# Changing the issue order of weight products, weight splits and one root in a decoder trunk on one core

## The chip, the cores and the metric

The kernel runs on one core of one Trainium2 chip. The metric is the device time of one execution in microseconds (us). Five engines matter here: PE (TensorE, matrix products), DVE (VectorE), ACT (ScalarE), POOL (GpSimd) and SP (SyncE), which issues most transfers. Each engine takes its instructions in the order in which the program was laid out for it.

## What is computed

A trunk of four decoder layers serves 256 prompt tokens and 8 x 4 sample tokens with the same weights, 288 token columns in all. Each layer is a feed-forward part, a token mixer and a second feed-forward part, each behind an RMS norm:

```python
for i in range(DEPTH):                       # 4 layers, mixer kind i % 3
    x = x + 0.5 * _swiglu(_rmsnorm(x, ...), ffn_w_in[i, 0], ffn_w_out[i, 0])
    h = _rmsnorm(x, norm_mix[i])
    # 0: sliding-window attention  1: gated delta net  2: gated linear recurrence (HGRN2)
    x = x + y
    x = x + 0.5 * _swiglu(_rmsnorm(x, ...), ffn_w_in[i, 1], ffn_w_out[i, 1])
```

The linear recurrence (layer 2) has 8 heads of width 128. Per head it computes decayed scores inside chunks of 32 tokens, carries a 128 x 128 state from chunk to chunk, and then normalises the head's output: `o * rsqrt(mean(o*o) + eps)`. All numbers are fp32; inputs and outputs are the trunk's rows, caches and states.

## The kernel before

**Weight products.** Activations lie transposed in SBUF, 128 features on the partitions and 288 tokens in the columns. Every weight matrix streams from HBM once, in chunks of 512 rows by 256 columns (four `raw` buffers). To keep fp32 accuracy with fp32r products, each 128-column piece of a chunk is split into a high part (`hi`, ACT, line 71) and the rest (`lo`, DVE, line 72); at most three pieces are split at a time. The activations are split in the same way. A job then covers up to four 128 x 128 blocks, and each block takes three products into the same PSUM tile: hi x high part of the activations (line 97), hi x low part (line 98), lo x high part (line 99). I call these the weight products: a job of four blocks has twelve, two blocks have six. `Stream.run` (line 85) emits the jobs; `Stream.split_to` (line 58) emits the splits two jobs ahead.

**Who decides the order.** The kernel is written against a scheduler that lays out each engine's queue when the program is built: it simulates the engines, and whenever an engine is free it takes the ready instruction of the best priority. Priority is the order of writing, and `tc.high_priority(n)` moves what is written under it n places ahead. `PRIO` is 5000 (line 107). So a weight product can be followed on PE by any other work that is ready and comes earlier in priority. On the chip the order is fixed: an instruction that waits holds up everything behind it on its engine.

**The mixers.** Their own work (scores, transposes, states) mixes with the weight products on PE. In attention (`swa`, line 398) it is written in the evacuations of the q jobs, so it precedes later products. In the recurrence (`hgrn`, line 1281) the 64 jobs of the input projections are written first, with the groups q0, f0, v0, f1, q1, v1, z0, z1 of four heads each; then `head_scores`, `head_states` and `gate` of the heads under `tc.high_priority(PRIO)`, then 8 output jobs after each half of the heads. The splits in this part have the priority of their place, because `st.first`, the places that line 70 moves them ahead, is 0. In the first part of the delta net it is `2 * PRIO`.

**Head norm.** In `head_states` ACT squares the head's output out of a PSUM tile with tag `c1` (line 1483), DVE makes mean plus eps (`gv`, line 1485), `root` (line 274) raises it to -0.5 on POOL (`gf`, one instruction, line 276), and ACT scales the output with it (line 1488), which also frees the PSUM tile. A second way to the same root exists, `rsqrt` (line 264): a bit trick and three Newton steps, two plus nine instructions on DVE, each of which reads what the one before it wrote. The feed-forward norms use it.

**The end of the recurrence.** `gate` (line 1503) multiplies each head's output with its gate z and splits the product for the output projection, whose 16 jobs are the last of this mixer.

```python
with self.tc.high_priority(self.first):                       # splits, line 70
    self.nc.scalar.activation(out=h, in_=src, func=AF.Copy)
...
for i, (xh, xl) in enumerate(xs):                             # products, line 96
    mm(ps, hi[:, i, :m], xh(), start=start and i == 0, stop=False)
    mm(ps, hi[:, i, :m], xl(), start=False, stop=False)
    self.mms.append(mm(ps, lo[:, i, :m], xh(), ...).ins)
```

Of the kernel before, what the change touches and what calls it, by code (L numbers as in the profile page):

```python
# [24 lines left out]
class Stream:  # L25
# [3 lines left out]
    def __init__(self, tc, raw, split, psum):  # L29
        self.tc, self.nc, self.raw, self.split_pool, self.psum = tc, tc.nc, raw, split, psum  # L30
        self.chunks, self.jobs = [], []
        self.loaded, self.tiles, self.left = 0, {}, {}
        self.nsplit, self.parts = 0, {}
        self.njob = 0
        self.accs = {}
        self.pooled = set()
        self.held, self.mms, self.tags = [], [], {}
        self.loads = {}
        self.first = 0

    def chunk(self, loads):
        self.chunks.append(loads)
# [42 lines left out]
    def run(self, count, hold=False):  # L85
        self.mms = []
        for j in range(self.njob, self.njob + count):
            self.split_to(j + 1 + AHEAD)
            chunk, view, nk, xs, acc, start, stop, evac, m = self.jobs[j]
            hi, lo = self.parts.pop(j)  # L90
            if start:
                self.accs[acc] = self.psum.tile([128, 512], F32, tag=self.tags.pop(acc, "acc"), name="acc")
            ps = self.accs[acc][:m, :T]
            mm = self.nc.tensor.matmul
            last = len(xs) - 1
            for i, (xh, xl) in enumerate(xs):
                mm(ps, hi[:, i, :m], xh(), start=start and i == 0, stop=False)  # L97
                mm(ps, hi[:, i, :m], xl(), start=False, stop=False)  # L98
                self.mms.append(mm(ps, lo[:, i, :m], xh(), start=False, stop=stop and i == last).ins)  # L99
            self.njob += 1  # L100
            if stop and hold:
                self.held.append((evac, self.accs.pop(acc)))
            elif stop:
                evac(self.accs.pop(acc))


PRIO = 5000
# [4 lines left out]
def trunk(ctx: ExitStack, tc: tile.TileContext, I, consts, O):  # L112
# [16 lines left out]
    st = Stream(tc, raw, split, Acc)  # L129
# [134 lines left out]
    def rsqrt(r, v, t):  # L264

        ri = r.bitcast(I32)
        V.tensor_single_scalar(ri, v.bitcast(I32), 1, ALU.logical_shift_right)
        V.tensor_scalar(ri, ri, -1.0, 1597463007.0, ALU.mult, ALU.add)
        for _ in range(3):
            V.scalar_tensor_tensor(out=t, in0=r, scalar=-0.5, in1=r, op0=ALU.mult, op1=ALU.mult)  # L270
            V.tensor_tensor(out=t, in0=t, in1=v, op=ALU.mult)
            V.scalar_tensor_tensor(out=r, in0=t, scalar=1.5, in1=r, op0=ALU.add, op1=ALU.mult)

    def root(r, v):

        G.tensor_tensor(out=r, in0=v, in1=roots[:v.shape[0]].to_broadcast(list(v.shape)), op=ALU.pow)  # L276
# [48 lines left out]
    def norm_run(key, halved):  # L325

        st.run(NJ, True)
        mms = st.mms
        with tc.high_priority(N1):
            if key[0] == "f" or key[1] in WIDE:  # L330
                with tc.issue_after(mms[NF]):
                    norm(key, halved)
            else:
                with tc.issue_after(mms[N0[0]]):
                    stats(key)
                newton(key)
                with tc.issue_after(mms[N0[1]]):
                    bcast(key, halved)
        st.flush()
# [941 lines left out]
    def hgrn(i, j):  # L1281
# [3 lines left out]
        q, k, f, z = (Slabs(F32) for _ in range(4))  # L1285
# [157 lines left out]
        def head_states(h):  # L1443

            H = L.pop(("h", h))
            sta, qb, bd, qm = H["sta"], H["qb"], H["bd"], H["qm"]
            vt = L["vt", h // 4][:, h % 4]
            s0 = slice(32 * (h % 4), 32 * (h % 4) + 32)
            vm = mx(1024, "vm", 1).rearrange("p (c n v) -> p c n v", c=2, n=4)
            SS = mx(1024, "SS", 2).rearrange("p (n v) -> p n v", n=8)  # L1450
            for c in range(2):
                for a in range(4):
                    S.activation(out=vm[:, c, a], in_=vt[:, c], func=AF.Copy, scale=L["blk"][:, a:a + 1])
            v4m = mx(1024, "v4m", 1, dt=F32R).rearrange("p (b v) -> p b v", b=8)
            for e in range(8):
                S.activation(out=v4m[:, e], in_=L["v4"][:, h], func=AF.Copy, scale=cc["m8"][:, e:e + 1])
            for c in range(2):
                ps = misc(("c1", "s")[c])
                PE.matmul(ps, H["kdt"][:, c * 128:c * 128 + 128], vm[:, c].rearrange("p n v -> p (n v)"))
                for a in range(4):  # L1460
                    n = 4 * c + a
                    if n == 0:
                        V.tensor_copy(out=SS[:, 0], in_=ps[:, 0:128])
                    else:
                        V.scalar_tensor_tensor(out=SS[:, n], in0=SS[:, n - 1], scalar=H["end"][:, n:n + 1],
                                               in1=ps[:, a * 128:a * 128 + 128], op0=ALU.mult, op1=ALU.add)
            nc.sync.dma_start(out=O[6][j, 0, h], in_=SS[:, 7])
            po = misc("c1")
            for c in range(2):
                PE.matmul(po[:, c * 128:c * 128 + 128], bd[:, c * 128:c * 128 + 128], vt[:, c], start=c == 0, stop=False)  # L1470
                for a in range(4):
                    n = 4 * c + a
                    if n:
                        PE.matmul(po[32 * a:32 * a + 32, c * 128:c * 128 + 128], qb[:, 32 * n:32 * n + 32], SS[:, n - 1],  # L1474
                                  start=False, stop=False)
            for e in range(8):
                a = e % 4
                PE.matmul(po[32 * a:32 * a + 32, 256:384], qm[:, 32 * e:32 * e + 32], sta[:, e], start=False, stop=False)
            PE.matmul(po[:, 256:384], bd[s0, 256:384], L["vs"][s0, h // 4], start=False, stop=True)
            ssq, v, r = sm(3, "gs"), sm(3, "gv"), sm(3, "gf")  # L1480
            o = mx(384, "o", 1)
            for c in range(3):
                S.activation(out=o[:, c * 128:c * 128 + 128], in_=po[:, c * 128:c * 128 + 128], func=AF.Square,
                             accum_out=ssq[:, c:c + 1])
            V.tensor_scalar(v, ssq, 1.0 / 128, EPS, ALU.mult, ALU.add)
            root(r, v)
            for c in range(3):
                S.activation(out=o[:, c * 128:c * 128 + 128], in_=po[:, c * 128:c * 128 + 128], func=AF.Identity,
                             scale=r[:, c:c + 1])
            for e in range(0, 8, 4):  # L1490
                ps = misc(("c1", "s")[e // 4])
                PE.matmul(ps, H["k4"], v4m[:, e:e + 4].rearrange("p b v -> p (b v)"))
                for a in range(4):
                    V.scalar_tensor_tensor(out=sta[:, e + a], in0=sta[:, e + a], scalar=H["ends"][:, (e + a) // 2, a % 2:a % 2 + 1],
                                           in1=ps[:, a * 128:a * 128 + 128], op0=ALU.mult, op1=ALU.add)
            nc.sync.dma_start(out=O[11][j, :, h].rearrange("b k v -> k b v"), in_=sta)
            ps = misc("s")
            for c in range(2):
                PE.transpose(ps[:, c * 128:c * 128 + 128], o[:, c * 128:c * 128 + 128], ident)
            PE.matmul(ps[:, 256:T], o[:, 256:384], L["lm"][:, 5])  # L1500
            S.activation(out=q[h], in_=ps[:, :T], func=AF.Identity, scale=hnorm)
# [19 lines left out]
        def run():  # L1521
            setup()
            norm_run(key, False)
            st.run(64 - NJ)
            for a in (0, 4):
                with tc.high_priority(PRIO):
                    if a == 0:
                        head_scores(0)
                    for h in range(a, a + 4):
                        if h < 7:  # L1530
                            head_scores(h + 1)
                        head_states(h)
                        gate(h)
                st.run(8)
        return run
    rows_y, turned = ((0, 128, 0), (128, 128, 0), (160, 128, 96)), {}

# [108 lines left out]
    ps = misc()  # L1646
# [11 lines left out]
    for k in range(9):  # L1658
        add_square(seq[0], k, G)
    for k, run in zip(seq, runs):  # L1660
        if k[0] == "f":
            run()
        else:
            with tc.tile_pool(name="mix", bufs=1, reuse_waits="tile") as M[0]:
                run()
# [92 lines left out]
```

## Time and profile before

| what | value |
|---|---|
| median of 3 runs | 2639.22 us (2635.47 to 2645.3) |
| the profiled execution's own time | 2632.71 us |
| its span, first to last instruction | 2630.9 us |
| mean granted TensorE clock | 0.989 of 2.4 GHz |
| attention of layer 0, delta net, recurrence, attention of layer 3 | about 228 to 345, 715 to 1150, 1620 to 1850, 2285 to 2400 us |

Engine rows of the profile's page give the busy time, its share of the span and the instructions. Matmuls overlap in the pipeline, so the time from the start of one product to the start of the next says more than the duration of one. Idle time of an engine is listed with what ended it. Clock shares are of 2.4 GHz; 0.5 is the lower level, 1.2 GHz.

### The profile page before, as it was taken

To read this page: it belongs to the slowest core of one execution; us is meant where nothing else is said; L and a number is where in the kernel's file an instruction comes from. 1 tells how busy PE (TensorE), PEld (TensorE's weight loads), DVE (VectorE), ACT (ScalarE), POOL (GpSimd) and SP (SyncE) were. 2 spreads that over 40 slices of the span, in tenths; PEclk is the share of its full clock that TensorE was granted. 3 is DMA by queue.
4 is the path that set the end of the run, shared out by engine and by line. 5 is a ranking of instruction groups with operands and counts; after the bars stand their busy time and mean duration, and the time that the engine had idled before them with its cause. 6 is when DMAs were issued, how large, how long until landed. Compare 5 with 4: busy or idle time off the path is not lost.

```text
span 2630.9 us, 52770 instructions
## 1 busy us (share of the span) xinstructions
PE 2549.8 (97%) x20268; PEld 2411.8 (92%) x20268; DVE 1763.5 (67%) x3772; ACT 1414.1 (54%) x3129; POOL 246.4 (9%) x404
## 2 busy tenths in 40 slices
PE   8999999999998899999999999888999999999998
PEld 8999799999997776789999999677999999979998
DVE  6666776576567867667666666877765766667655
ACT  5555655455455456755555545665554555465543
POOL 1000000000002135410000000443000000010000
PEclk9999999999999999999999999999999999999999
DMA  6655245555553354455555555333555565534553
GB/s 188 196 168 172 65 143 164 165 168 161 166 163 97 109 152 136 136 176 159 167 163 163 168 163 160 106 119 122 164 165 164 164 202 177 168 94 121 161 168 124
DMA packets 442609, 400.15 MB, mean 152 GB/s; under 512 B 24730, under 2 KB 440212, under 8 KB 442356
## 3 DMA queue, kind: packets, MB, share of 16 engines
q1 hardware_dynamic: 441732, 395.66, 49.9%
q8 instruction: 159, 2.61, 0.4%
q10 hardware_dynamic: 624, 1.11, 0.1%
q14 instruction: 94, 0.77, 0.1%
HBM read 374.64 MB, written 22.07 MB: 151 GB/s over the span
## 4 chain that ended last, share of the span: by engine, by line
PE 78%; issue 11%; DVE 6%; POOL 2%; ACT 2%; DMA 1%; DVEq 0%; POOLq 0%; ACTq 0%; SPq 0%
PE acc L97 23%; PE acc L99 23%; PE acc L98 23%; DVE lo L72 1%; PE s L545 1%; PE c L530 1%; PE c L1186 0%; DVE W L1400 0%; PE ma L537 0%; PE c L1190 0%; DVE F L1366 0%; PE c L1192 0%; PE c L1181 0%; PE c L1474 0%; ACT hi L71 0%
## 5 line engine op out<-in xcount | busy, mean ns | idle before, releaser
L97 PE MATMUL acc<-sl,hi 128*128 128x288 f32 x5384 | 1612.4, 300 | 13.0 <-ACT sl L1506 2.8
L98 PE MATMUL acc<-sl,hi 128*128 128x288 f32 x5384 | 1606.1, 298 | 1.8 <-DVE sl L1507 1.8
L99 PE MATMUL acc<-sl,lo 128*128 128x288 f32 x5384 | 1600.8, 298 | 2.4 <-DVE lo L72 2.4
L71 ACT ACTIVATE hi<-raw 128x512 fp32r<-128x512 f32 (+1 forms) x1378 | 854.3, 621 | 963.0 <-PE acc L98 934.4
L72 DVE TENSOR_TENSOR lo<-raw,hi 128x512 fp32r<-128x512 f32 (+1 forms) x1378 | 948.4, 689 | 571.2 <-ACT hi L71 515.1
L97 PEld LDWEIGHTS acc<-sl,hi 128*128 128x128 f32 x5384 | 1016.4, 189 | 26.2 <-issue 11.5
L99 PEld LDWEIGHTS acc<-sl,lo 128*128 128x128 f32 x5384 | 1021.2, 190 | 14.6 <-issue 10.0
L98 PEld LDWEIGHTS acc<-sl,hi 128*128 128x128 f32 x5384 | 1018.9, 189 | 12.8 <-issue 9.2
L276 POOL TENSOR_TENSOR r<-v,roots 128x3 f32<-128x3 f32 x5 | 5.8, 1164 | 1847.2 <-DVE v L296 1847.2
L366 DVE TENSOR_TENSOR sil<-acc,sil 128x288 f32<-128x288 f32 x176 | 79.7, 456 | 54.8 <-PE acc L99 51.3
L359 DVE TENSOR_TENSOR sil<-acc,rbc 128x288 f32<-128x288 f32 x176 | 79.6, 456 | 50.1 <-PE acc L99 49.8
L368 DVE TENSOR_TENSOR sl<-sil,sl 128x288 fp32r<-128x288 f32 x176 | 78.9, 452 | 0.0
L360 ACT ACTIVATE sil<-sil 128x288 f32<-128x288 f32 x176 | 77.6, 445 | 2.1 <-DVE sil L359 2.0
L367 ACT ACTIVATE sl<-sil 128x288 fp32r<-128x288 f32 x176 | 77.6, 445 | 0.0
L700 DVE SCALAR_TENSOR_TENSOR acc<-buf,cw,acc 128x312 f32<-128x312 f32 x96 | 59.0, 625 | 11.9 <-ACT acc L698 11.5
L246 ACT ACTIVATE sl<-x,gT 128x288 fp32r<-128x288 f32 x96 | 51.0, 536 | 26.2 <-DVE x L383 15.3
L249 DVE SCALAR_TENSOR_TENSOR sl<-x,gT,sl 128x288 fp32r<-128x288 f32 x96 | 50.5, 530 | 0.1
L262 ACT ACTIVATE sq<-x 128x288 f32<-128x288 f32 x91 | 38.7, 430 | 5.1 <-DVE x L383 5.1
L515 ACT ACTIVATE e<-e,m 128x128 f32<-128x128 f32 (+1 forms) x72 | 32.6, 454 | 16.1 <-DVE m L512 15.8
L1131 POOL TENSOR_TENSOR st<-st,ex 128x512 f32<-128x512 f32 x32 | 37.4, 1190 | 18.1 <-PE ma L1098 18.1
L259 DVE TENSOR_TENSOR ssq<-ssq,sq 128x288 f32<-128x288 f32 x84 | 37.8, 450 | 0.1
L512 DVE CUSTOM_DVE_ANT_0 e<-c,sl,sink 128x128 f32<-128x128 f32 (+1 forms) x72 | 27.8, 418 | 10.6 <-PE c L530 7.7
(435 smaller groups left out, 1823.3 us busy)
## 6 DMA issues: line engine op xcount, KB each, us to landing
raw<-in_ffn_w_in_dram SPq DMA_DIRECT2D x352, 512.0 KB
raw<-in_ffn_w_out_dram SPq DMA_DIRECT2D x128, 512.0 KB
raw<-in_ffn_w_out_dram SPq DMA_DIRECT2D x64, 384.0 KB
raw<-in_gdn_w_in_dram SPq DMA_DIRECT2D x48, 512.0 KB
raw<-in_hgrn_w_in_dram SPq DMA_DIRECT2D x32, 512.0 KB
out_dram<-st SPq DMA_DIRECT2D x24, 512.0 KB
raw<-in_swa_w_in_dram SPq DMA_DIRECT2D x32, 256.0 KB
raw<-in_swa_w_out_dram SPq DMA_DIRECT2D x32, 256.0 KB
```

Of the source, the lines that this page charges most:

```text
L71: self.nc.scalar.activation(out=h, in_=src, func=AF.Copy)
L72: (self.nc.gpsimd if j in self.pooled else self.nc.vector).tensor_tensor(out=l, in0=src, in1=h, op=ALU.subtract)
L97: mm(ps, hi[:, i, :m], xh(), start=start and i == 0, stop=False)
L98: mm(ps, hi[:, i, :m], xl(), start=False, stop=False)
L99: self.mms.append(mm(ps, lo[:, i, :m], xh(), start=False, stop=stop and i == last).ins)
L246: S.activation(out=h[m], in_=x[:, m], func=AF.Identity, scale=g)
L359: V.tensor_tensor(out=t, in0=ps[:, :T], in1=nrm[key]["rbc"], op=ALU.mult)
L360: S.activation(out=t, in_=t, func=AF.Silu)
L366: V.tensor_tensor(out=t, in0=ps[:, :T], in1=t, op=ALU.mult)
L367: S.activation(out=h, in_=t, func=AF.Copy)
L368: V.tensor_tensor(out=l, in0=t, in1=h, op=ALU.subtract)
L700: V.scalar_tensor_tensor(out=a[:, 0:312], in0=b[:, t:t + 312], scalar=cw[:, 32 * t + mt:32 * t + mt + 1], in1=a[:, 0:312], op0=ALU.mult, o ...
```

## The change

Three edits. First, `Stream` gets a number `follow`, set for each part of the trunk: 0 in the delta net, `3 * PRIO` everywhere else. Of the two blocks of a pair, the first product keeps its priority, and the five behind it are moved `follow` places ahead. Second, in the recurrence `st.first` is `2 * PRIO` from the run of the last 56 of the 64 input jobs to the end of the part, so the splits are ahead of the heads' work (which is ahead by `PRIO`) on ACT and DVE. Third, the head norm of the recurrence takes its root with `rsqrt` on DVE in place of `root` on POOL; the squares' tile `ssq` is its scratch.

```diff
-        self.first = 0
+        self.first = self.follow = 0
...
             for i, (xh, xl) in enumerate(xs):
-                mm(ps, hi[:, i, :m], xh(), start=start and i == 0, stop=False)
-                mm(ps, hi[:, i, :m], xl(), start=False, stop=False)
-                self.mms.append(mm(ps, lo[:, i, :m], xh(), start=False, stop=stop and i == last).ins)
+
+                with self.tc.high_priority(i % 2 * self.follow):
+                    mm(ps, hi[:, i, :m], xh(), start=start and i == 0, stop=False)
+                with self.tc.high_priority(self.follow):
+                    mm(ps, hi[:, i, :m], xl(), start=False, stop=False)
+                    self.mms.append(mm(ps, lo[:, i, :m], xh(), start=False, stop=stop and i == last).ins)
...
             V.tensor_scalar(v, ssq, 1.0 / 128, EPS, ALU.mult, ALU.add)
-            root(r, v)
+            rsqrt(r, v, ssq)
...
             norm_run(key, False)
+            st.first = 2 * PRIO
             st.run(64 - NJ)
...
                 st.run(8)
+            st.first = 0
         return run
...
     for k, run in zip(seq, runs):
+        st.follow = 0 if k[0] == "m" and k[1] % 3 == 1 else 3 * PRIO
```

## Rows read from the trace of the kernel before

**Rows 1.** The page's engine part: busy us (share of the span) and instructions.

```profile
PE 2549.8 (97%) x20268; PEld 2411.8 (92%) x20268; DVE 1763.5 (67%) x3772; ACT 1414.1 (54%) x3129; POOL 246.4 (9%) x404
```

**Rows 2.** Stretches: us, busy (instructions) of PE, PEld, DVE, ACT, POOL; clock, DMA, GB/s.

```profile
228.00:345.00 117.00, 113.97 (x867) 96.19 (x866) 79.50 (x262) 65.23 (x185) 12.47 (x21) 0.96 0.36 97
350.00:510.00 160.00, 160.00 (x1199) 159.69 (x1198) 105.34 (x191) 83.95 (x154) 0.00 (x0) 1.00 0.53 163
1620.00:1850.00 230.00, 200.85 (x2139) 169.91 (x2139) 177.90 (x416) 141.07 (x410) 83.85 (x109) 0.96 0.40 122
```

**Rows 3.** PE's waits in the recurrence: us in total, times, longest us.

```profile
PE c L1415 <- DVE W L1400: 5.7, 4, 3.0
PE c L1415 <- POOL W L1400: 5.5, 2, 2.9
PE acc L97 <- ACT sl L1506: 2.8, 1, 2.8
PE acc L99 <- DVE lo L72: 2.2, 3, 0.9
PE acc L98 <- DVE sl L1507: 1.8, 1, 1.8
```

**Rows 4.** PE's timeline, 301 to 304 us (attention): start us, us, instruction.

```profile
300.95 0.29 PE L99 MATMUL acc<-sl,lo 128*128 128x288 f32 x1
301.22 0.43 PE L545 MATMUL s<-pt,m 128*64 128x128 f32 x2
301.58 0.55 PE L537 MATMUL ma<-cst,e 128*128 128x128 f32 x3
301.88 0.38 PE L97 MATMUL acc<-sl,hi 128*128 128x288 f32 x1
302.10 0.30 PE L98 MATMUL acc<-sl,hi 128*128 128x288 f32 x1
...
302.63 0.29 PE L99 MATMUL acc<-sl,lo 128*128 128x288 f32 x1
302.85 0.87 PE L545 MATMUL s<-pt,m 128*64 128x128 f32 x10
303.65 0.55 PE L537 MATMUL ma<-cst,e 128*128 128x128 f32 x3
...
304.17 0.30 PE L98 MATMUL acc<-sl,hi 128*128 128x288 f32 x1
```

**Rows 5.** PE's timeline: first and last break of the products in the three mixers.

```profile
235.34 0.72 PE L291 MATMUL ma<-ones,ssq 128*128 128x1 f32 x6
...
2386.80 0.42 PE L572 MATMUL s<-pt,vc 128*64 128x32 f32 x4
```

**Rows 6.** A stretch of the recurrence, as rows 2: the first two heads' scores.

```profile
1645.00:1670.00 25.00, 18.07 (x295) 16.39 (x294) 24.06 (x48) 11.81 (x30) 16.59 (x22) 0.86 0.23 71
```

**Rows 7.** Sources L1300 and L1505, DVE: ns min/median/max, first and last start us.

```profile
L1300 DVE TENSOR_TENSOR q<-acc,rbc x16: 445/456/458, 1635.8 to 1829.4; 128x288 f32<-128x288 f32 x16
...
L1505 DVE TENSOR_TENSOR og<-sl x4: 446/1044/1058, 1830.5 to 1835.7; 128x288 f32<-128x288 f32 x4
```

**Rows 8.** The head norm: source L276 on POOL, and one head's DVE and ACT timeline.

```profile
L276 POOL TENSOR_TENSOR gf<-gv,roots x8: 850/850/854, 1680.4 to 1817.3; 128x3 f32<-128x3 f32 x8
...
1715.07 0.16 DVE L1485 TENSOR_SCALAR gv<-gs 128x3 f32<-128x3 f32 x1
...
1716.26 0.37 ACT L1488 ACTIVATE o<-c,gf 128x128 f32<-128x128 f32 x1 [0.45 <-POOL gf L276]
```

**Rows 9.** DVE's timeline in attention: two small instructions, the second reads the first.

```profile
267.51 0.16 DVE L518 TENSOR_TENSOR rs<-rs,es 128x2 f32<-128x2 f32 x1 [0.24 <-ACT es L517]
267.70 0.17 DVE L519 RECIPROCAL rs<-rs 128x2 f32<-128x2 f32 x1
```

**Rows 10.** DVE's timeline in the first feed-forward norm: a split between two `rsqrt` steps.

```profile
25.30 0.68 DVE L72 TENSOR_TENSOR lo<-raw,hi 128x512 fp32r<-128x512 f32 x1
25.91 0.45 DVE L271 TENSOR_TENSOR sq<-sq,ssq 128x288 f32<-128x288 f32 x1
```

## The prediction

> **What bounds the kernel now.** I begin with the engines' busy shares [rows 1]: PE is busy 97% of the span, so only PE's order, its idle time and what it loses between instructions can move the time. Next come the stretches [rows 2]. In a feed-forward stretch PE has no idle time: 160 us hold 1199 instructions, nearly all products, 0.133 us from one to the next. There the products follow each other already, so the first edit finds nothing to gather, and these parts (about 1700 of the 2631 us) should keep their time. What is left is two attentions and the recurrence; the delta net has `follow` 0. Attention idles little, 117.0 - 114.0 = 3.0 us. The recurrence idles 230.0 - 200.9 = 29.1 us, with the clock at 0.96 on average, so part of it ran at 1.2 GHz. Its waits [rows 3] say on what: 5.7 + 5.5 = 11.2 us for the `W` tiles of the heads' scores, 2.8 + 1.8 = 4.6 us at the gates, only 2.2 us for a late split.
>
> What ends the recurrence is the last gate job of the input projection. Its evacuation is at 1829.4 us and the first gate multiplies at 1830.5 [rows 7], although heads 0 to 3 were long done; the last head's root is at 1817.3 [rows 8]. So the heads finish 12 us ahead of the products: the products, last in priority, are the late ones, and the heads have slack. The worst place is the first two heads' scores [rows 6]: DVE busy 24.1 of 25 us, PE 18.1 at a clock of 0.86. The DVE queue runs the heads' work ahead of the splits there, so PE's queue was laid out with few products to put between the scores, and on the chip it stands in front of a score whose `W` is late.
>
> **Edit 1, runs of six.** A product costs 0.133 us wherever it stands; what can be saved is the cost of leaving the products and coming back. In attention [rows 4], from L99 at 300.95 to L98 at 302.10 are 1.15 us with two product steps (0.27), three transposes L537 (301.58 to 301.88, 0.10 each) and two L545. The next break, 302.63 to 304.17, takes 1.54 us and has eight L545 more, so one L545 is 0.39 / 8 = 0.05. Left for the break itself: 1.15 - 0.27 - 0.30 - 0.10 = 0.48 us.
>
> How many breaks go? In the three stretches PE's timeline has 176 places where other work stands between two products (48, 77 and 51; the first and the last are [rows 5]). With five of six products moved ahead by three times `PRIO`, a break can only fall between pairs. 61 of the 176 lie in the same pair as the break before, and would merge with it. In about 20 of those both sides hold the dearer kind, L545 or state work; a merge with a break of transposes alone I count at nothing, as its own cost isn't separable. So 20 x 0.48 = -9.6, taken as **-9 us**. Ends: 0, if the scheduler puts the gathered work elsewhere, and 61 x 0.48 = -29. What it costs: a head's PE step that becomes ready inside a pair waits for up to five products, 0.67 us. In the recurrence the 12 us of slack cover that. In attention other products cover it; if they ran out, the step would be bare, and I leave that to the range.
>
> First the row on coming back: L97 after a break takes 0.22 us to the next product instead of 0.13 (301.88 to 302.10 in [rows 4]). The Trainium skill, TensorE: Matmul & The Clock Gate, Part 2 (Step-by-step: what each phase is for), says PE pulls a weight load ahead of running matmuls, so by it alone a return would be covered. The trace doesn't bear that out here, where the return costs 0.09 us more.
>
> **Edit 2, splits first.** 56 input jobs and 16 output jobs get their ACT and DVE split ahead of the heads. No instruction is added; 0.68 us of DVE per split [rows 10] moves forward, past the heads' DVE work, and the raw buffer is returned earlier, so SP's next load too. DVE has 230.0 - 177.9 = 52 us free in the stretch [rows 2]. What is late next: the heads' `W`, `F` and states, behind at most two splits at a time, as there are three split buffers; and the evacuations of the input jobs stay behind the heads, with three accumulators to fill. The prize is the idle time up to the last gate job, 29.1 - 4.6 = 24.5 us, plus some of the low clock. Ends: -24, and +11, if the waits for `W` double because the scores come later on DVE. I take **-10**, somewhat under half of the prize, since rows 6 show DVE itself nearly full where PE idles most: there a split ahead is a score behind. The heads' scores can afford it, as the products of v0 and then f1, q1, v1 are what their next steps need.
>
> **Edit 3, the root.** Now `gv` starts at 1715.07 and ACT's scaling at 1716.26 [rows 8], 1.19 us with 0.85 us of POOL. After: eleven dependent DVE instructions on 128 x 3. The nearest rows are two dependent instructions on 128 x 2, 0.19 us from start to start [rows 9], so 0.19 + 11 x 0.19 = 2.3 us: +1.1 us per head and 9 us over eight heads, behind which wait the scaling, the transposes and the next use of the `c1` tile. That fits in the 12 us of slack, and 8 x 2.1 = 17 us of DVE fit in the 52. I charge **+2** for splits and evacuations that stand behind a root. Ends: -7, if POOL's 8 x 0.85 us held up `W` tiles queued behind them, and +50: a split between any two steps adds 25.91 - 25.30 = 0.61 us [rows 10], (1.1 + 11 x 0.61) x 8 = 62, less 12 of slack.
>
> That is a price by row, and a page has a lower one. The Trainium skill, VectorE: DVE Perf Modes (The TRN2 errata), states 58 cycles at 0.96 GHz plus the columns, by which I estimate 0.064 us a step and 0.7 us for eleven. By that the root would be shorter than POOL's and the term about -2, which would put the time at 2618. Rows 9 have 0.16 and 0.17 us for such an instruction, and no overlap between dependent ones.
>
> **The sum.** -9 - 10 + 2 = -17 us against the profiled execution's own 2632.7 (its span is 2630.9): 2615.7. The median of the runs shown is 2639.2, 6.5 above that execution, so I predict **2622** us, 0.65% below the median. A measurement of this kernel can tell about 0.5%, 13 us, from no change.
>
> **Rivals.**
> - *The waits only change their names.* PE still meets each late `W` in order, because a split ahead delays the scores as much as it feeds PE, and edit 2 gives nothing; the root eats half of what the runs give. -9 + 5 = -4: 2635. For it: DVE at 24.1 of 25 us in [rows 6], and only 2.2 us of split waits in [rows 3]. Against it: the 12 us by which the products come last. Chance 0.22.
> - *A break is free.* If the gathered work pays the same entry and return as before (in groups by tile rather than per break), edit 1 is 0 and -10 + 2 = -8 remains: 2631. That is what the pulled-ahead weight load of the page above would make of it. [Rows 4] speak against it; that three transposes beside a break take no more than 0.10 each speaks for it. Chance 0.11.
> - *The root becomes the end, slower.* The splits rank above the root on DVE and can go between its steps, as in [rows 10]. It decides where a head's chain grows by over 12 / 8 = 1.5 us; 1.1 is spent already, so one split per root is enough. With six splits among eleven steps it is 1.1 + 3.7 = 4.8 us a head, 38 in all, 26 over the slack; with the runs' -9 that is +17: 2656. For it: the 0.61 us in [rows 10]. Against it: only two splits can be ready ahead, and a split comes once per 1.6 us of products (12 x 0.133). Chance 0.15.
>
> **How the numbers follow.** The forecast has 0.52; its own range is 2604 (all of the idle time goes) to 2626. The first two rivals lie within 13 us of 2639: same 0.33. The third is slower, 0.15. For eight in ten the range runs from 2604 to 2655, just short of the slow rival's price.
>
> **What would show it.** Right: in attention and the recurrence the products stand in multiples of six, with some 115 breaks for 176; the feed-forward stretch keeps 1199 instructions in 160 us; the last q evacuation comes some 15 us earlier in the recurrence than 1829.4; PE's waits for `W` fall under 6 us; in [rows 6]'s place PE is busier at a higher clock. `rsqrt` shows eleven steps of about 0.19 us. Wrong: PE waits for the scaled head output or for the states grow past 10 us and the gates wait for the last head instead of the last evacuation; or the recurrence keeps its 230 us with other names on the waits; or a feed-forward part changes its time, which nothing here explains.

## The result: slower, and the profile after

The changed kernel takes 2660.8 us (median of 5 runs, 2655.46 to 2674.94) where the kernel before takes 2639.22: ratio 1.0082, 95% interval [1.0062, 1.0101]. I had forecast 2622, in a range up to 2655. The profiled execution is the slowest of the five, 2674.94 us with a span of 2673.1, 14 us above its median; the one of before is 6.5 us below its own. So the two profiled spans differ by 42.2 us where the medians differ by 21.6. The diff shifts the lines of the code: what was L97, L98, L99 is now L99, L101, L102, and later lines move by 3. The experiments' kernels keep the lines of before.

First the engines on the page of the changed kernel, beside [rows 1]:

```profile
PE 2577.5 (96%) x20268; PEld 2431.2 (91%) x20268; DVE 1761.8 (66%) x3860; ACT 1409.9 (53%) x3129; POOL 232.7 (9%) x396
```

PE has the same 20268 instructions and is busy 28 us longer. DVE has 88 more instructions (11 for each of 8 heads) and POOL 8 fewer, so the root did move. Next come the stretches of the parts, each from its first weight product to the first of the next part. Columns are as in [rows 2]; what PE is not busy is its idle time. Before (attention of layer 0, delta net, recurrence, attention of layer 3):

```profile
230.54:353.58 123.04, 120.01 (x913) 102.23 (x911) 86.35 (x278) 70.87 (x198) 12.47 (x21) 0.96 0.37 102
777.68:1200.30 422.62, 394.70 (x3491) 326.84 (x3490) 302.71 (x784) 249.66 (x715) 129.39 (x243) 0.98 0.48 137
1623.55:1862.46 238.91, 209.76 (x2206) 178.82 (x2205) 187.55 (x438) 148.96 (x427) 83.85 (x109) 0.96 0.40 123
...
2285.97:2406.43 120.46, 117.64 (x913) 100.54 (x911) 85.52 (x278) 71.77 (x199) 13.04 (x19) 0.97 0.36 101
```

After, and a feed-forward stretch that answers to the second of [rows 2]:

```profile
230.78:350.00 119.22, 116.70 (x912) 100.71 (x911) 87.13 (x279) 70.72 (x198) 13.28 (x21) 0.97 0.38 106
350.00:510.00 160.00, 160.00 (x1199) 159.66 (x1198) 103.79 (x187) 82.81 (x152) 0.00 (x0) 1.00 0.53 164
774.16:1235.06 460.90, 422.97 (x3491) 345.02 (x3490) 296.68 (x783) 250.47 (x714) 122.35 (x243) 0.90 0.45 125
1658.31:1902.13 243.82, 209.75 (x2206) 179.37 (x2205) 199.85 (x525) 148.28 (x425) 77.60 (x101) 0.94 0.40 121
...
2326.40:2448.92 122.52, 120.43 (x913) 103.08 (x911) 85.79 (x279) 72.50 (x199) 11.83 (x19) 0.93 0.36 99
```

**Nearly all of the loss is in the delta net, the part I had left out of the sum.** It grows from 422.6 to 460.9 us: 38.3 of the 42.2 us between the two profiled executions. Its PE runs as many instructions (3491). Of the 38.3 us, 37.9 - 27.9 = 10.0 are idle time and 28.3 are PE busy for longer, at a mean clock of 0.90 for 0.98. The recurrence, where most of my 17 us were to come from, takes 4.9 more. The feed-forward stretch keeps its 1199 instructions.

Inside the delta net the time is lost in two places. Here is the middle of it before, by 50 us:

```profile
950.00:1000.00 50.00, 47.69 (x393) 34.84 (x392) 37.82 (x93) 36.15 (x127) 27.99 (x48) 1.00 0.57 162
1000.00:1050.00 50.00, 46.96 (x374) 34.72 (x375) 36.84 (x88) 32.36 (x118) 28.51 (x48) 1.00 0.47 128
1050.00:1100.00 50.00, 47.56 (x387) 35.43 (x385) 35.63 (x87) 34.44 (x117) 23.09 (x36) 1.00 0.56 156
```

And after, with the two worst stretches by themselves:

```profile
950.00:1000.00 50.00, 47.69 (x338) 33.50 (x336) 31.04 (x79) 31.67 (x111) 19.88 (x38) 0.86 0.36 99
1000.00:1050.00 50.00, 43.64 (x289) 30.95 (x285) 24.92 (x62) 25.21 (x90) 20.99 (x36) 0.76 0.41 112
1050.00:1100.00 50.00, 44.34 (x288) 30.48 (x287) 25.65 (x63) 25.33 (x85) 16.04 (x29) 0.74 0.43 120
...
1005.00:1033.00 28.00, 23.57 (x123) 15.10 (x121) 11.98 (x29) 12.39 (x45) 9.44 (x16) 0.58 0.45 124
1066.00:1093.00 27.00, 21.81 (x125) 13.82 (x123) 12.09 (x29) 11.65 (x43) 10.37 (x19) 0.65 0.43 118
```

PE's timeline at both ends of the first of them:

```profile
1005.08 0.29 PE L102 MATMUL acc<-sl,lo 128*128 128x288 f32 x1
1005.21 0.40 PE L1143 MATMUL ma<-w,km 128*128 128x256 f32 x2
1007.22 0.74 PE L1143 MATMUL ma<-w,km 128*128 128x256 f32 x4 [1.61 <-POOL km L1138]
...
1032.14 1.12 PE L1184 MATMUL c<-co,sl 128*64 128x128 f32 x8
1033.19 0.44 PE L1189 MATMUL c<-vt,sl 64*64 64x128 f32 x4
1033.56 0.40 PE L99 MATMUL acc<-sl,hi 128*128 128x288 f32 x1
```

Between the product at 1005.08 and the one at 1033.56 there is none: 28.5 us of heads' work alone. A second such hole, 27.0 us, begins at 1066. Before, the longest hole in this part is 10.2 us. The product at 1033.56 has no wait in brackets: it wasn't late, it stands there in the queue. In the hole PE waits for what came in time before (1.61 us for `km` here; in the whole part 6.5 us for 1.8), and the granted clock is at 0.58 there, the work taking longer too: a burst of eight L1184 lasts 1.12 us. The same eight before, on the timeline at a clock of 1.00:

```profile
963.44 0.66 PE L1181 MATMUL c<-co,sl 128*64 128x128 f32 x8
```

PE's waits for `km` in the whole part, after and then before:

```profile
PE ma L1143 <- POOL km L1138: 6.5, 6, 1.6
```

```profile
PE ma L1140 <- POOL km L1135: 1.8, 4, 0.6
```

### The profile page after: what moved, and what is told of

The parts are those of the page before. It is cut to its first block, busy times and chain, and to the rows that moved or that the text cites. A ratio compares the mean times of both kernels' runs of the same rounds, so it can differ in the third digit from the quotient of the medians.

```text
span 2673.1 us, 52870 instructions
## 1 busy us (share of the span) xinstructions
PE 2577.5 (96%) x20268; PEld 2431.2 (91%) x20268; DVE 1761.8 (66%) x3860; ACT 1409.9 (53%) x3129; POOL 232.7 (9%) x396
## 4 chain that ended last, share of the span: by engine, by line
PE 41%; issue 10%; DVE 4%; ACT 0%; DMA 0%; POOL 0%; DVEq 0%; POOLq 0%; ACTq 0%
PE acc L99 13%; PE acc L102 12%; PE acc L101 12%; DVE lo L72 1%; DVE W L1403 1%; DVE F L1369 0%; PE c L1477 0%; PE c L533 0%; PE c L1473 0%; DVE SS L1468 0%; PE s L548 0%; DVE st L1497 0%; PE ma L540 0%; PE s L575 0%; ACT hi L71 0%
## 5 line engine op out<-in xcount | busy, mean ns | idle before, releaser
L99 PE MATMUL acc<-sl,hi 128*128 128x288 f32 x5384 | 1622.4, 302 | 22.8 <-DVE sl L1223 6.7
L101 PE MATMUL acc<-sl,hi 128*128 128x288 f32 x5384 | 1596.2, 297 | 0.0
L102 PE MATMUL acc<-sl,lo 128*128 128x288 f32 x5384 | 1593.1, 297 | 0.3 <-DVE lo L72 0.3
L99 PEld LDWEIGHTS acc<-sl,hi 128*128 128x128 f32 x5384 | 1018.8, 189 | 45.4 <-issue 25.2
L102 PEld LDWEIGHTS acc<-sl,lo 128*128 128x128 f32 x5384 | 1021.0, 190 | 5.2 <-issue 3.8
L101 PEld LDWEIGHTS acc<-sl,hi 128*128 128x128 f32 x5384 | 1019.6, 190 | 6.4 <-issue 5.1
L703 DVE SCALAR_TENSOR_TENSOR acc<-buf,cw,acc 128x312 f32<-128x312 f32 x96 | 50.6, 552 | 10.1 <-ACT acc L701 9.9
L385 DVE TENSOR_TENSOR res<-acc,rh 128x288 f32<-128x288 f32 x64 | 29.1, 454 | 40.7 <-PE acc L102 40.7
L262 DVE TENSOR_TENSOR ssq<-ssq,sq 128x288 f32<-128x288 f32 x84 | 37.9, 451 | 0.1
```

The lines of the kernel that those rows point to most:

```text
L703: V.scalar_tensor_tensor(out=a[:, 0:312], in0=b[:, t:t + 312], scalar=cw[:, 32 * t + mt:32 * t + mt + 1], in1=a[:, 0:312], op0=ALU.mult, o ...
```

## Experiments

Each ratio is against the kernel before, run beside it on the same chip (medians 2639.6 to 2641.4 us over the batches); an interval is 95%. A part's length is that of its stretch as above, in one profiled execution. A *break* is a place where other work stands between two products. Of the diffs only the lines that matter are shown, cut with `...`; `follow` and `first` are set inside neighbouring lines in the kernels, to the same effect.

A length from one profile has a spread of its own. The delta net's PE order is that of before in 13 of the traces, and there it takes 422.2 to 429.1 us, with 27 to 28 us of idle time and a mean clock of 0.980 down to 0.960. The first attention takes 122.8 to 126.0 us in ten traces with the same order, at 0.958 down to 0.932. The recurrence takes 238.9 to 239.5 us in four.

### Why does the delta net change at all?

Before, nothing stood around the products. After, the delta net's products stand under `tc.high_priority(0)`. Moving what stands under it is not all that this bracket does. On entry the bracket sets the scheduler's counter back by n; on leaving it sets it to what it was on entry. So products under it, even with n = 0, don't use up places, and the products of following jobs and the heads' work between them get other ranks than before.

**e1: the bracket of 0 places, in the delta net alone.** Nothing else of the change is in it.

```diff
+    ahead = lambda self, n: nullcontext() if self.follow is None else self.tc.high_priority(n)
...
-                mm(ps, hi[:, i, :m], xh(), start=start and i == 0, stop=False)
+                with self.ahead(i % 2 * (self.follow or 0)): mm(ps, hi[:, i, :m], xh(), ...)
...
+        st.follow = 0 if k[0] == "m" and k[1] % 3 == 1 else None
```

> The kernel before, with one thing added: in the delta net each weight product stands under a priority bracket of 0 places, as the change has it there. No runs of six, no splits ahead, root on POOL. Theory A (a bracket of 0 places is not nothing: leaving it sets the order counter back, so all products of several jobs get one priority and jobs interleave in the delta net): its PE order there is that of the changed kernel, the delta net takes 455 to 465 us instead of 423, the median is 2660 to 2675, and the clock stands at 1.2 GHz for 60 us or more in that part. Theory B (the delta net of the changed kernel is slow because of what comes before it, a shift of attention or of the transfers): 423 us there, median 2635 to 2645.

Measured: 2670.01 us, 1.0112 [1.0093, 1.0132]; the delta net takes 455.1 us. The bracket that moves nothing by its number costs 30 us by itself. The order isn't quite that of the changed kernel, as I had expected, but both are slow. In this kernel's trace one sees what it does first: two jobs run into each other.

```profile
782.49 0.51 PE L97 MATMUL acc<-sl,hi 128*128 128x288 f32 x2
782.84 0.42 PE L98 MATMUL acc<-sl,hi 128*128 128x288 f32 x2
783.10 0.42 PE L99 MATMUL acc<-sl,lo 128*128 128x288 f32 x2
```

Each kind comes twice in a row here, where before the order in this part was L97, L98, L99 with four exceptions. The breaks fall from 153 to 122, and the longest holes are 28.3 and 28.1 us.

**e2: the whole change, without the bracket in the delta net.**

```diff
-        st.follow = 0 if k[0] == "m" and k[1] % 3 == 1 else 3 * PRIO
+        st.follow = None if k[0] == "m" and k[1] % 3 == 1 else 3 * PRIO
```

> The changed kernel, with the delta net's products written without any bracket; runs of six, splits ahead and the root as changed elsewhere. Theory A: delta net back at 422 to 424 us, first attention about -4, recurrence about +5, second attention about +2 against before, so 2640 to 2646. Theory B: delta net at 450 or more, 2655 to 2670.

Measured: 2635.8 us, 0.9985 [0.9972, 0.9997]; the delta net 425.1 us. So 25 of the changed kernel's 2660.8 us hang on this bracket. It also shows that the rest of the change is worth almost nothing, which the third group takes up.

**e3: e1, with the counter advanced by a job's products once a job is written.**

```diff
-            self.njob += 1
+            self.njob += 1; self.tc.cur_priority += 0 if self.follow is None else 3 * len(xs)
```

> As the first run, but after each job of the delta net the counter is moved on by as many places as the job has products, so products share a priority within a job but not across jobs. If the interleaving of two jobs is what costs: delta net within 5 us of 423, median 2635 to 2645. If the shared priority within a job (or the bracket as such) costs: 440 us or more there, median over 2652.

Measured: 2648.09 us, 1.0031 [1.002, 1.0042]; the delta net 431.0 us, 153 breaks, longest hole 11.6 us. With the places given back the long holes are gone, and most of the loss with them. Neither branch is met: some loss stays, with 34.8 us of idle time in the part, and within a job the products still share a rank. What that remainder comes from was not settled.

**e12: the whole change, with a bracket that leaves the counter where the products would have left it.**

```diff
+    @contextmanager
+    def ahead(self, n):
+        p = self.tc.cur_priority; self.tc.cur_priority = p - n; yield; self.tc.cur_priority += n
```

> The whole change, with a bracket that leaves the scheduler's counter where the products would have left it; the delta net has this bracket with 0 places, as the change has the library's. If the rewound counter is the cause and not a bracket as such: the delta net at 423 to 428 us and the whole at 0.996 to 1.000. If any bracket around the products costs the delta net its time: 455 us there, ratio 1.008 to 1.011.

Measured: 2641.05 us, 1.0001 [0.9991, 1.0012]; the delta net, where this bracket has 0 places, stands in the order of before and takes 428.1 us, within the spread of that order. It isn't a bracket as such that costs the time, but the counter that is set back. The total is no clean measure of that alone, as the counter is kept in the other parts too; the recurrence takes 246.8 us here.

**e4: the library's bracket of 0 places in every part.**

```diff
+        st.follow = 0
```

> The kernel before with the bracket of 0 places around every product in every part, so that two jobs interleave in the feed-forward parts as well, where nothing else stands between products. If interleaved products cost by themselves (a late split, an accumulator that comes free late): feed-forward parts of 215 us or more instead of 211.6, 8 of them, +30 us and more beside the delta net's. If interleaving costs only where the supply of products must be spread between other work: feed-forward 211 to 213 us, delta net about +38.

Measured: a single execution, 2679.56 us, so without an interval; the delta net 452.9 us, and each of the eight feed-forward parts 1.7 to 2.1 us longer. A feed-forward stretch, first of this kernel, then of the one before:

```profile
60.00:220.00 160.00, 160.00 (x1189) 158.65 (x1187) 97.86 (x187) 80.04 (x148) 0.00 (x0) 1.00 0.58 183
```

```profile
60.00:220.00 160.00, 160.00 (x1199) 159.61 (x1198) 100.42 (x187) 82.05 (x149) 0.00 (x0) 1.00 0.61 187
```

Ten products fewer in 160 us, with PE busy throughout. Even where there is nothing but products, the changed ranks cost 0.8%, in the delta net 452.9 / 422.6, 7%. In this stretch jobs run into each other too, and 22 steps from one product to the next take 0.19 to 0.24 us, where before 3 do; why these steps are longer was not settled. In the changed kernel, where the bracket has `3 * PRIO` in the feed-forward parts, the products keep their order there but for a few, and the eight parts add up to 1700.4 us for 1699.9.

**e16: runs of six in the delta net too** (`follow` at `3 * PRIO` in all three mixers), with the root on DVE and without splits first, as in e13 below. Here the products are gathered in the order of the jobs.

> As e13, and the delta net's products in runs of six as well, in the order of the jobs. If gathering is good there too and the loss came from the mixed jobs alone: the delta net 415 to 424 us (153 breaks become 88), ratio 0.987 to 0.991, the lowest of all. If what costs the delta net its time is that products are taken together and leave the heads' work bare: 430 us or more, PE idle over 30 us and a longer stretch at the lower clock, ratio above 0.993.

Measured: 2659.25 us, 1.0066 [1.0049, 1.0083]; the delta net 468.7 us. There are only 88 breaks, and holes of 28.3 and 29.2 us some 9 us later than in the changed kernel; the first of them:

```profile
1014.00:1042.00 28.00, 23.74 (x124) 15.24 (x123) 11.14 (x28) 13.33 (x47) 9.33 (x18) 0.58 0.42 115
```

So it doesn't take jobs that run into each other to lose the time: here they don't, and more is lost. What e1, e16 and the changed kernel share is that products are taken early and are missing later. Counted in the traces: when product 864 of this part's 1560 is done, the heads have done 1132 of their 1927 PE instructions in the changed kernel, in e1 and in e16, but 1333 before, in e3 and in e12. In all three slow kernels the first long hole stands between products 864 and 865 and the second between 960 and 961. What keeps product 865 back until then was not settled. In this part a break is no loss but the cover of the heads' work. The counter is set back in e16 as well, so no run shows what runs of six would do here with the counter kept.

### What is each edit worth alone?

**e5: runs of six in the recurrence alone**, no bracket elsewhere.

```diff
+        st.follow = 3 * PRIO if k[0] == "m" and k[1] % 3 == 2 else None
```

> The kernel before with runs of six in the recurrence alone. By the prediction's term (breaks between products cost 0.2 to 0.5 us each, some twenty costly ones merge): recurrence -3 to -6 us against 238.9, median 2634 to 2637. Rival (a step of a head that becomes ready inside a pair waits up to 0.67 us, and the heads are on the path): recurrence +2 us or more, median 2642 or more.

Measured: 2629.59 us, 0.9961 [0.995, 0.9972]; the recurrence 231.7 us, its idle time 24.5 for 29.1, its breaks 56 for 77. The part is 7.2 us shorter, more than the 3 to 6 expected.

**e8: runs of six in the two attentions alone.**

```diff
+        st.follow = 3 * PRIO if k[0] == "m" and k[1] % 3 == 0 else None
```

> The kernel before with runs of six in the two attention parts alone. By the prediction's term: 48 and 51 breaks become about 30 each, -2 to -3 us per attention at the same share of the lower clock, median 2633 to 2638. Rival (longer stretches of small work between the runs lower the clock, which gives it back): attention parts within 1 us of before or longer, and more time at 1.2 GHz in them than the 17 us of before.

Measured: 2633.07 us, 0.9978 [0.9969, 0.9988]; breaks 30 for 48 and 27 for 51. The two parts take 120.6 and 122.5 us in the profile, the second 2 us longer than before, but at a clock of 0.930 for 0.972; with the order of before it takes 124.5 us at 0.931 (e3). At like clocks both attentions are 2.0 to 2.5 us shorter, as expected.

**e6: splits first alone.**

```diff
             norm_run(key, False)
+            st.first = 2 * PRIO
...
                 st.run(8)
+            st.first = 0
```

> The kernel before with the weight splits of the recurrence ahead of the heads' work, nothing else. By the prediction's term: recurrence -10 us (ends -24 and +11), PE's waits for the scores' W tiles under 6 us. Rival (a split ahead delays the scores as much as it feeds PE): recurrence within 3 us of 238.9, the waits for W and for the scores' result at 10 us or more.

Measured: 2639.5 us, 0.9993 [0.9983, 1.0003]. PE's waits for `W` add up to what they were, 11.0 us for 5.7 + 5.5 in [rows 3], now all of them on DVE:

```profile
PE c L1415 <- DVE W L1400: 11.0, 7, 3.0
```

That is my first rival to the letter: the waits only change their names.

**e7: the root on DVE alone.**

```diff
-            root(r, v)
+            rsqrt(r, v, ssq)
```

> The kernel before with the head norm's root in eleven VectorE instructions, nothing else. By the prediction: +1.1 us on each head's chain, eight heads, mostly inside the heads' slack: recurrence 0 to +4 us. Rival (the root becomes the end, with splits between its steps): +10 us or more. Second rival (POOL is freed and the next heads' W tiles come sooner): -3 us or less, waits of PE for POOL's W near 0.

Measured: 2636.04 us, 0.9988 [0.9979, 0.9997]; the recurrence 235.2 us. A small gain, not a cost.

### Why don't the gains add?

Runs alone take the recurrence to 231.7 us and the root alone to 235.2, but with all three edits (e2) it takes 241.5.

**e10: runs and root in the recurrence. e11: runs and splits there.** From here on the kernels join the edits of e5 to e8; no line is new.

> Runs of six in the recurrence alone, with VectorE's root, without splits first. With all three edits the recurrence took 241.5 us, with the runs alone 231.7. If the root beside the runs is what gives the gain back: ratio about 0.999, the recurrence near 240 us, PE waiting for the heads' scores or outputs. If the root stays as good beside the runs as it was alone (3.7 us): 0.995, the recurrence 228 to 232 us, POOL no longer among what ends PE's waits for W.

> Runs of six in the recurrence alone, with splits first, without VectorE's root. If it is the splits that give the gain of the runs back (a split ahead on DVE delays a score, and behind the score now stand up to five gathered products): ratio 0.998 to 1.000, the recurrence 238 to 242 us with over 32 us of PE idle, most of it waits for W, at and o. If the splits are as harmless beside the runs as alone: 0.996, the recurrence near 232 us.

Measured: e10 2624.21 us, 0.9941 [0.9927, 0.9954], the recurrence 222.7 us. e11 2630.44 us, 0.996 [0.9946, 0.9973], the recurrence 228.3 us. Neither pair gives the gain back.

**e14: splits and root, no runs. e15: all three in the recurrence, the attentions as before.**

> Splits first and VectorE's root in the recurrence, no runs of six anywhere. If splits and root hurt each other (a split stands between the steps of a root, my slow rival): the recurrence 240 us or more, ratio 1.000 to 1.002, and the root's eleven steps stretched by splits between them. If they only hurt together with the runs: near 234 us, 0.998.

> All three edits in the recurrence, the attentions and the delta net as before. If the order in the recurrence itself gives the gain back: 240 to 247 us there with 34 us or more of PE idle, ratio 0.999 to 1.001. If it was the attention's runs ahead of it: 222 to 230 us, 0.994 to 0.996.

Measured: e14 2640.58 us, 0.9997 [0.9988, 1.0006], 239.9 us, so neither branch quite: the root's small gain no longer shows, though the interval overlaps that of e7, and there is no loss. e15 2641.28 us, 1.0005 [0.9994, 1.0015], 243.2 us with 34.8 of idle time. It is the recurrence's own order, not the attention ahead of it, that loses the gain of the runs, and it takes splits *and* root.

**e9: runs in attentions and recurrence. e13: the same with the root, so the whole change but the splits and the brackets of the delta net and the feed-forward parts.**

> Runs of six in the two attentions and in the recurrence, no bracket around any other product, no splits first, POOL's root. If the gains of the single parts stand side by side (0.39% from the recurrence alone, 0.22% from the attentions alone): ratio 0.994, about 2623 us, the recurrence about 232 us, the attentions about 121 and 122, the delta net at its 423 us. If one part's gain depends on how the part before it ends, or on the state of the clock that it hands on: 0.996 to 0.998, and the recurrence back near 239 us.

> Runs of six in the attentions and the recurrence, VectorE's root, no splits first, no bracket in the delta net. If it is the splits that spoil the three together: the recurrence 222 to 226 us as with runs and root alone, the attentions 119 and 121, ratio 0.990 to 0.993, about 2617 us, under both kernels. If the attention ahead or the number of edits at work is what gives the gain back: the recurrence near 240 us, 0.996 to 0.998.

Measured: e9 2622.75 us, 0.9937 [0.9923, 0.995]. e13 2617.84 us (2613.48 to 2621.01), **0.9907 [0.9891, 0.9923]: faster than both kernels.** Its recurrence, beside that of before and after above:

```profile
1628.19:1850.24 222.05, 202.72 (x2207) 174.85 (x2205) 191.15 (x525) 148.29 (x427) 78.25 (x101) 0.98 0.43 130
```

Two lines tell which side ends this part: the last q evacuation for the products, as in [rows 7], and the `gv` of the last head's norm for the heads, as in [rows 8]. In the changed kernel:

```profile
L1303 DVE TENSOR_TENSOR q<-acc,rbc x16: 443/454/460, 1669.0 to 1844.9; 128x288 f32<-128x288 f32 x16
...
L1488 DVE TENSOR_SCALAR gv<-gs x8: 159/163/267, 1716.2 to 1883.9; 128x3 f32<-128x3 f32 x8
```

And in e13:

```profile
L1300 DVE TENSOR_TENSOR q<-acc,rbc x16: 443/449/459, 1638.9 to 1810.5; 128x288 f32<-128x288 f32 x16
...
L1485 DVE TENSOR_SCALAR gv<-gs x8: 159/160/168, 1682.8 to 1830.2; 128x3 f32<-128x3 f32 x8
```

Counted from the first product of the part:

| kernel | last q evacuation | last `gv` | length |
|---|---|---|---|
| before | 205.8 | 193.5 | 238.9 |
| e6, splits | 204.2 | 197.7 | 237.4 |
| e5, runs | 199.3 | 189.0 | 231.7 |
| e7, root | 196.2 | 213.6 | 235.2 |
| e13, runs and root | 182.3 | 202.0 | 222.0 |
| e14, splits and root | 188.9 | 220.6 | 239.9 |
| changed kernel, all three | 186.6 | 225.6 | 243.8 |

Before, the products end last, 12 us after the heads. With the root on DVE it is the other way round: the heads end last, by 17 us in e7 and 20 in e13. Splits first put DVE to work for the products at the heads' expense. Where the heads are the late side, that buys nothing and delays what ends last: by 225.6 - 202.0 = 24 us between e13 and the changed kernel, with the products no earlier. PE's waits in the recurrence say on what, first e13, then the changed kernel:

```profile
PE c L1415 <- DVE W L1400: 4.1, 5, 2.9
PE c L1470 <- DVE SS L1465: 3.6, 4, 1.2
...
PE c L1436 <- DVE at L1422: 1.0, 2, 0.9
```

```profile
PE c L1439 <- DVE at L1425: 8.6, 6, 1.7
PE c L1418 <- DVE W L1403: 6.8, 6, 2.3
...
PE s L1502 <- ACT o L1491: 4.3, 2, 3.7
PE c L1473 <- DVE SS L1468: 4.3, 7, 1.2
```

## Why the prediction was wrong, step by step

The medians of four kernels, built up from the kernel before, give the sum as it is. They come from different batches, whose kernels before differ by up to 2 us. The step to e2 also brings the brackets of `3 * PRIO` in the feed-forward parts, which e13 lacks; these parts add up to 1700.4 us in e13 and 1700.7 in e2, so the step is that of the splits.

| step | us | this step | I had said |
|---|---|---|---|
| before | 2639.6 | | |
| runs in attentions and recurrence (e9) | 2622.75 | -16.9 | -9 |
| root on DVE (e13) | 2617.84 | -4.9 | +2 |
| splits first (e2) | 2635.8 | +18.0 | -10 |
| bracket of 0 places in the delta net (changed kernel) | 2660.8 | +25.0 | nothing |

- **The step that failed: "What is left is two attentions and the recurrence; the delta net has `follow` 0."** I read 0 places as no change and put the part at nothing. The products there came under a bracket that they hadn't had, which sets the counter back, and the part costs 25.0 us more with it (the changed kernel against e2). With the other terms as they are, it turns a kernel that is 0.15% faster into one that is 0.8% slower. It stood in no rival and not in my list of what would prove me wrong.
- **Edit 1: mechanism right, term too low.** In the changed kernel's attentions and recurrence all products stand in runs of at least six, with 30 + 60 + 27 = 117 breaks for the 115 said. In e9, 18 + 21 + 24 = 63 went, for the 61 merges counted. I gave a price to 20 of them only. Spread over all, a break that went is worth 16.9 / 63 = 0.27 us, between the bound of 0 and the 0.48 of [rows 4], inside the ends 0 and -29. By part it is 6.6 / 42 = 0.16 us in the attentions (e8), where I had read the 0.48, and 10.1 / 21 = 0.48 us in the recurrence (e5), of which 4.6 us in all are less idle time. So the price was too high where I read it and the count of dear breaks too low. The rival "a break is free" is out: the runs alone gain 16.9 us. These brackets set the counter back too, and no run parts that from the gathering.
- **Edit 2: the term with the wrong sign.** Alone it is the rival "the waits only change their names" (e6). The last q evacuation does come earlier in the changed kernel, by 205.8 - 186.6 = 19 us where I had said some 15, but e13 gets there without splits, at 182.3. The waits for `W`, to fall under 6 us, are 8.2 for the 11.2 in [rows 3] (6.8 on DVE, 1.4 on POOL). In [rows 6]'s place PE is no busier, 18.0 of 25 us for 18.1, though the clock is 0.93 for 0.86. The 12 us of slack on which I sent the splits ahead were the very slack that I also let the root spend. I added two terms that draw on one reserve.
- **Edit 3: wrong sign, well inside its ends.** I had the root's length about right where no split stands between its steps. The last head of the changed kernel, the first and the last two steps:

```profile
1883.88 0.17 DVE L1488 TENSOR_SCALAR gv<-gs 128x3 f32<-128x3 f32 x1
...
1886.10 0.16 DVE L274 TENSOR_TENSOR gs<-gs,gv 128x3 f32<-128x3 f32 x1
1886.30 0.16 DVE L275 SCALAR_TENSOR_TENSOR gf<-gs,gf 128x3 f32<-128x3 f32 x1
```

  That is 2.58 us to the end, for 2.3 said, with 0.20 us from the last step but one to the last. The estimate of 0.7 us for eleven steps, from the Trainium skill's 58 cycles plus the columns (VectorE: DVE Perf Modes, The TRN2 errata), is not borne out; the same section says that this row comes out too short for a single instruction, and the 0.16 us of a step here agrees. With two or three splits and some evacuations between the steps it is 4.5 to 5.9 us for the other heads, as the slow rival had it; but in e13 it is 4.8 to 7.7 us and the kernel gains. In e7 the heads' last `gv` comes 213.6 - 193.5 = 20 us later, where I had counted 9. The gain lies towards the low end that I named, but the reason that I gave for that end is not shown. PE's waits for a `W` from POOL are 5.5 us in [rows 3] and 1.2 in e7, but they are gone in e9 already, where the root still stands on POOL. What falls with the root is the sum of the waits for `W`, from 9.1 + 2.0 = 11.1 us in e9 to 4.1 + 2.0 + 0.5 = 6.6 in e13. How the root brings that about was not settled. In e9, and the two lines of e13 that are not shown above:

```profile
PE c L1415 <- DVE W L1400: 9.1, 7, 2.9
...
PE c L1415 <- ACT W L1393: 2.0, 1, 2.0
```

```profile
PE c L1415 <- ACT W L1393: 2.0, 1, 2.0
...
PE c L1415 <- POOL W L1400: 0.5, 1, 0.5
```

- **The slow rival** ("the root becomes the end") was right about the recurrence and wrong about the kernel. The heads do end last, by 225.6 - 186.6 = 39 us. That takes the gain of the runs (e15 against e5: 2641.28 to 2629.59) and not 17 us more. Its 2656 is near the measured time by a mechanism that isn't the one at work.

What is shown: the bracket is the cause (e1, e2), through the counter that it sets back (e3, e12), and the long holes go with it (e1 and e16 against e3). What is argued only: that the lower clock in the holes follows from the heads' work standing alone there, and how much of the 38.3 us is the clock's. The clock was not held by itself; the rows show the two together, in two kernels.

## What to carry to other kernels

Ask of each line that a change wraps, even with a factor of 0, whether the order of the built queue stays the same, and compare the orders part by part before pricing anything: a part that the description leaves out can still carry the result. Two edits that both spend the slack of one chain must be summed on that chain, not each by itself; find out which side ends last after the first before adding the second. Gathering products paid in the attentions and the recurrence here (e8, e5). In the delta net, where many small dependent steps need cover, it cost time (e16 against e13, 2659.25 to 2617.84 us), though with brackets that also set the counter back.

## What was not expected of the hardware

- In 28 us without a product the granted clock is 0.58 on average, although PE is busy for 23.57 of them; afterwards it is at 1.00 again at once in one case (1033.50 to 1048.00) and still at 0.50 in the other (1093.50 to 1110.00):

```profile
1033.50:1048.00 14.50, 12.57 (x104) 9.49 (x101) 9.02 (x24) 8.44 (x30) 10.06 (x19) 1.00 0.42 113
...
1093.50:1110.00 16.50, 16.50 (x80) 11.23 (x81) 5.14 (x17) 6.40 (x22) 6.08 (x13) 0.50 0.37 103
```

- The same order of instructions takes different times with the clock: five executions of the changed kernel gave 2674.94 us at a mean clock of 0.972, 2660.8 at 0.977 and 2655.46 at 0.982. A profile of one execution can so be 14 us off its median, a third of the 42.2 us between the two profiles.
